# Layer 1's attention by key head, in 64 fixed steps that are filled with projections

## The chip, the core and the metric

One Trainium2 chip, one of its cores. The core has a matrix engine (TensorE, called PE here), a vector engine (DVE), a scalar engine (ACT), GpSimd (POOL) and SyncE (SP, which issues most DMAs here). The operands lie in SBUF, the results of PE in PSUM. The metric is the time of one execution on the device in microseconds (us); the kernel before takes 1667.85 us, the median of three runs (1666.11 to 1668.38).

## What is computed

A two-layer encoder over 512 tokens of width 1024. Each layer is a token mixer, a normalisation, then a mixture of 32 experts of which every token uses two. Layer 0's mixer is neighbourhood attention and is the same in both kernels. Layer 1's mixer, which the change rewrites, is grouped-query attention: 16 query heads of 64 share 4 key heads, so one key head serves four query heads.

```
def gqa_mixer(h, cos, sin, w_qkv, q_gain, k_gain, w_o):
    B, S, D = h.shape
    kvd = GQA_KV_HEADS * HEAD_DIM
    qkv = h @ w_qkv
    q = qkv[..., :D].reshape(B, S, N_HEADS, HEAD_DIM)
    k = qkv[..., D:D + kvd].reshape(B, S, GQA_KV_HEADS, HEAD_DIM)
    v = qkv[..., D + kvd:].reshape(B, S, GQA_KV_HEADS, HEAD_DIM)
    q = apply_axial_rope(rms_norm(q, q_gain), cos, sin)
    k = apply_axial_rope(rms_norm(k, k_gain), cos, sin)
    return block_gqa_attention(q, k, v) @ w_o
...
        s = jnp.einsum('bqkgd,bskd->bkgqs', qb, k).astype(jnp.float32) * scale
        p = jax.nn.softmax(s, axis=-1).astype(v.dtype)
        return jnp.einsum('bkgqs,bskd->bqkgd', p, v)
...
        x = layer_norm(DEEPNORM_ALPHA * x + (1 + g1) * y, ln_g[i, 0], ln_b[i, 0])
        h = x * (1 + sc2) + sh2
        y = hierarchical_moe(h, moe_w_group[i], moe_b_group[i], moe_w_expert[i], moe_b_expert[i],
                             moe_w_gate[i], moe_w_up[i], moe_w_down[i])
        x = layer_norm(DEEPNORM_ALPHA * x + (1 + g2) * y, ln_g[i, 1], ln_b[i, 1])
```

## The kernel before

Tokens come in four blocks `t` of 128; X[t] is a block of the residual, 128 tokens by 1024. Products that need more than one pass of the engine's precision are made of three: a weight or an activation is split into a high and a low part (`wh`/`wl`, `hTH`/`hTL`, `oH`/`oL`), the high part by a copy on ACT (L312 in `split`, L467 in `split_wo`), the low part by a subtraction on POOL or DVE (L313, L469), and PE makes high by high, high by low and low by high. Whoever splits a weight therefore gives ACT a copy and POOL a subtraction.

Layer 1 in order, with the time at which each part starts in the profile:

- From 872.9 us, `mixer1` (L718): eight steps `k` transpose a piece of the hidden state and multiply it with the first half of the key and value weights into four accumulators named `pj` (PSUM, four buffers), 12 matmuls a step; then `proj(("kv", 1))` makes the values with another 96 matmuls.
- From 906 us, four times `proj(("q1", c))`, 96 matmuls each, one for each key head `c`. `rope` (L764) takes every accumulator to SBUF on ACT and DVE, `root` (L779) makes the factor of the RMS norm on DVE and ACT, and `queries` (L808) multiplies, splits (`hf`), transposes and copies to `qS` (named w in the trace, L820). The old residual is scaled by two rows (`pg`, `pb`, broadcast by PE into PSUM) on DVE in the same stretch (L834, L835, two of them for each half of a block).
- From 981.5 us, `attention(t)` (L847) for each block `t`: 16 tiles a block, each two score matmuls (`ps`), the row maximum on DVE (`st`, L860), the exponential on ACT (`pr`, L862), four transposes on PE (`pt`) and a copy of them to SBUF (`PT`) by ACT (L869) or DVE (L867), half each. After eight tiles the probabilities multiply the values (`po`), and `scaled` (L882) divides by the sums `rz` (`rze` transposed on PE, `rzb` copied by ACT). `split_wo` (L452) is called after the first block's code, with four steps of four ACT copies and four POOL subtractions. `project(t - 1)` (L976) multiplies the block before with the output weights (`pw`, 48 matmuls), adds it to X, transposes X and makes the router's logits; `router(t - 1)` follows.
- At 1164.4 us the first expert's `gate_up` (L1375, `gu`) begins, and the mixture of experts fills the rest to 1651 us.

The order in which PE takes all this in layer 1's mixer is not written out: the list scheduler of the language interleaves the blocks by its own costs. In the mixture of experts PE's order is the program's (`manual_schedule`, L1284), SP's order is the program's everywhere. SP loads weights into slots of 1 MB (`W`, L242), a slot being free once the last reader of its weights is done.

Of the kernel before, what the change touches and what calls it, by code (L numbers as in the profile page):

```python
# [8 lines left out]
F32 = mybir.dt.float32  # L9
# [8 lines left out]
P = 128  # L18
# [16 lines left out]
NWY = (3, 1)  # L35
# [30 lines left out]
class Trunk:  # L66
# [15 lines left out]
    def plan(self):  # L82
# [50 lines left out]
        for l in range(DEPTH):  # L133
# [5 lines left out]
            for h in range(2):  # L139
                for kh in range(2):  # L140
                    add(("wo", l, h, kh), a["wo"][l, h, kh])
            for h in range(2):
                for kh in range(2):
                    add(("wl", l, h, kh), None)
# [307 lines left out]
    def split_wo(self, l, pool):  # L452
        nc = self.nc
        self.nh, self.wh = self.slots(l, pool), pool
        hk = [(h, kh) for h in range(2) for kh in range(2)]
# [262 lines left out]
    def mixer1(self, st, qS):  # L718
        nc, a, tc = self.nc, self.a, self.tc
        qv = st.enter_context(tc.tile_pool(reuse_waits="tile", name="qv1", bufs=1))  # L720
        kHL = [qv.tile([P, 4, S], F32R, name=n) for n in ("kHH", "kLL")]
        V = qv.tile([P, NT, 256], F32, name="V")
        with tc.tile_pool(reuse_waits="tile", name="m1", bufs=1) as pool, tc.tile_pool(reuse_waits="tile", name="m1p", bufs=2, space=PSUM) as pp:
            rt = pool.tile([P, 4, NT, HD], F32, name="rt")
            nc.scalar.dma_start(rt[:, 0:2], a["rope"])
            gn = pool.tile([P, 4, HD], F32, name="kk", bufs=6)
            for i in range(4):
                nc.scalar.dma_start(gn[:, i, :], bcast(a["gain"][i:i + 1], [P, HD]))
            for i in (2, 3, 0, 1):
                nc.gpsimd.tensor_tensor(rt[:, i], rt[:, i % 2], bcast(gn[:, i:i + 1, :], [P, NT, HD]), op=OP.mult)  # L730
            hH = pool.tile([P, KD, S], F32R, name="hTH")
            hL = pool.tile([P, KD, S], F32R, name="hTL")
            c1 = pool.tile([P, 2, KD], F32, name="c1")
            self.fold_cols(c1[:, 0], c1[:, 1], self.lnc[:, 0, 2], self.lnc[:, 0, 3], self.col[1][:, 0], self.col[1][:, 1])
            w = self.W(("kv", 0))
            whl = [self.split(pool, w[:, 1024 * x:1024 * x + 1024], [P, 1024], 4, (nc.vector, None)[x]) for x in range(2)]
            acc = [pp.tile([P, 4, HD], F32, name="pj", bufs=4) for t in range(NT)]
            for k in range(KD):
# [51 lines left out]
            def keys():  # L790
                r = root(ks.rearrange("p a b -> p (a b)"), 1.0, NT, "rs")
                for t in range(NT):
                    nc.vector.tensor_tensor(kk[t], kk[t], bcast(r[:, t, :, None], [P, 4, HD]), op=OP.mult)
                    kd = pool.tile([P, 2, 4, 2, HD], F32R, name="kd", bufs=1)
                    for d in range(2):
                        nc.scalar.activation(kd[:, 0, :, d, :], kk[t], AF.Copy)
# [28 lines left out]
            for c in range(4):  # L825
# [11 lines left out]
                for t, ps in proj(("q1", c)):  # L837
# [3 lines left out]
                    if t == QPOST:  # L841
                        post()
# [793 lines left out]
```

## Time and profile before

| | us |
|---|---|
| median of three runs | 1667.85 |
| the profiled execution, its own time | 1673.29 |
| its span | 1671.6 |
| PE busy in the span | 1574.7 (94%) |
| DVE busy | 700.6 (42%) |
| ACT busy | 437.6 (26%) |
| POOL busy | 162.3 (10%) |
| layer 1's mixer, first matmul to first `gu` | 872.9 to 1164.4 |

All stretches are in us from the start of the span. A busy PE is not a PE at its peak: matmuls are pipelined, and a row's duration overlaps the next row, so the price of a matmul is read from the start of one row to the start of the next. The names left and right of the arrow are tiles of the program, output first. Line numbers are those of the kernel before.

### The profile page before, as it was taken

How to read it: one execution, taken by the hardware profiler on the slowest of the kernel's cores; microseconds unless marked ns; L12 is line 12 of the kernel's file. 1: busy time of each engine (PE TensorE's matmuls, PEld its weight loads, DVE VectorE, ACT ScalarE, POOL GpSimd, SP SyncE). 2: the span in 40 equal slices, each digit the busy share in tenths (PEclk: the TensorE clock that was granted, in tenths of full speed). 3: DMA queues.
4: the chain of work that ended last, by engine and by line, in shares of the span. 5: the costliest groups of instructions: out<-in, count | busy, mean ns of one | idle time of the engine just before them, and what ended most of it. 6: DMA issues, size and time to landing. Idle time of an engine off the chain costs nothing. (4 is left out here: it accounts for less than half of the span.)

```text
span 1671.6 us, 21362 instructions
## 1 busy us (share of the span) xinstructions
PE 1574.7 (94%) x8490; PEld 906.6 (54%) x8490; DVE 700.6 (42%) x1605; ACT 437.6 (26%) x934; POOL 162.3 (10%) x99
## 2 busy tenths in 40 slices
PE   7899997989999999999979989998999999999995
PEld 4676664773544545455448866766354545545442
DVE  3434545574232322323256865666432232323235
ACT  2343335231110111111134475453011111101112
POOL 2322212010000000000014250011000000000001
PEclk9999997999999999999989989999999999999997
DMA  9587872357999999999932000035899999999981
GB/s 328 196 309 269 331 306 104 137 202 295 417 419 420 419 419 420 419 419 420 420 125 102 26 1 25 1 125 206 368 416 420 420 420 420 419 420 420 419 332 51
DMA packets 76198, 493.17 MB, mean 295 GB/s; under 512 B 9876, under 2 KB 11284, under 8 KB 18876
## 3 DMA queue, kind: packets, MB, share of 16 engines
q1 hardware_dynamic: 71916, 485.05, 71.4%
q10 hardware_dynamic: 4176, 6.69, 1.2%
q8 instruction: 69, 1.13, 0.3%
q14 instruction: 37, 0.30, 0.1%
HBM read 489.61 MB, written 2.10 MB: 294 GB/s over the span
## 5 line engine op out<-in xcount | busy, mean ns | idle before, releaser
L300 PE MATMUL gu<-w,xT 128*64 128x512 f32 x2048 | 445.0, 592 | 0.0
L300 PEld LDWEIGHTS gu<-w,xT 128*64 128x64 f32 x2048 | 146.8, 137 | 291.6 <-issue 287.0
L300 PE MATMUL pd<-w,hx 128*64 128x512 f32 x1024 | 228.0, 598 | 0.0
L1391 DVE TENSOR_TENSOR h<-h,gu 128x512 f32<-128x512 f32 x32 | 22.0, 688 | 370.4 <-PE gu L300 370.4
L300 PEld LDWEIGHTS pd<-w,hx 128*64 128x64 f32 x1024 | 70.9, 137 | 140.3 <-issue 136.7
L300 PE MATMUL gc<-OH,zH 128*128 128x256 f32 x480 | 121.5, 291 | 2.6 <-DVE OH L1276 2.6
L300 PE MATMUL gc<-OH,zL 128*128 128x256 f32 x480 | 118.6, 284 | 0.0
L300 PE MATMUL gc<-YH,OT 128*128 128x512 f32 x244 | 104.2, 427 | 1.0 <-DVE X L1358 1.0
L1358 DVE TENSOR_TENSOR X<-X,gc 128x512 f32<-128x512 f32 x128 | 87.4, 688 | 39.3 <-PE gc L300 39.3
L300 PEld LDWEIGHTS gc<-OH,zH 128*128 128x128 f32 x480 | 92.5, 193 | 14.9 <-issue 11.4
L300 PE MATMUL gc<-YL,OT 128*128 128x512 f32 x244 | 96.3, 394 | 0.0
L300 PEld LDWEIGHTS gc<-OH,zL 128*128 128x128 f32 x480 | 92.6, 193 | 0.0
L300 PE MATMUL pw<-w,oH 128*128 128x512 f32 x256 | 86.3, 408 | 0.0
L1414 ACT ACTIVATE YH<-h 128x512 fp32r<-128x512 f32 x32 | 20.2, 630 | 233.6 <-DVE h L1413 233.6
L300 PE MATMUL pj<-wh,hTH 128*128 128x256 f32 (+1 forms) x272 | 71.2, 304 | 9.1 <-ACT hTH L419 4.0
L1294 ACT ACTIVATE xT<-gc,A 128x256 f32<-128x256 f32 x60 | 33.8, 566 | 173.9 <-PE gc L300 173.9
L300 PE MATMUL pj<-wl,hTH 128*128 128x256 f32 (+1 forms) x272 | 68.0, 292 | 0.0
L300 PE MATMUL pj<-wh,hTL 128*128 128x256 f32 (+1 forms) x272 | 65.6, 293 | 0.8 <-DVE hTL L427 0.8
L300 PEld LDWEIGHTS gc<-YH,OT 128*128 128x128 f32 x244 | 45.8, 188 | 37.3 <-DVE X L1358 15.8
L1292 DVE TENSOR_SCALAR xT<-gc,A 128x256 f32<-128x256 f32 x60 | 32.5, 545 | 76.9 <-ACT xT L1294 76.5
L1390 ACT ACTIVATE h<-gu 128x512 f32<-128x512 f32 x32 | 19.1, 597 | 173.0 <-PE gu L300 173.0
L303 PE MATMUL pt<-c_ident,pr 128*128 128x128 f32 x384 | 59.5, 283 | 2.1 <-ACT pr L862 2.0
(345 smaller groups left out, 2355.9 us busy)
## 6 DMA issues: line engine op xcount, KB each, us to landing
w<-in_gu SPq DMA_DIRECT2D x256, 1024.0 KB, 14.3
w<-in_dn SPq DMA_DIRECT2D x128, 1024.0 KB, 13.5
w<-in_ada SPq DMA_DIRECT2D x40, 1024.0 KB, 7.9
wq<-in_wqk SPq DMA_DIRECT2D x16, 512.0 KB, 3.6
w<-in_wo SPq DMA_DIRECT2D x8, 1024.0 KB, 5.8
w<-in_adaq SPq DMA_DIRECT2D x6, 1024.0 KB, 12.0
bias<-in_nab ACTq DMA_DIRECT2D x24, 256.0 KB, 3.4
w<-in_wq SPq DMA_DIRECT2D x4, 1024.0 KB, 4.9
```

The lines of the kernel that those rows point to most:

```text
L300: return self.nc.tensor.matmul(out, l, r, start=start, stop=stop, **kw)
L303: self.nc.tensor.transpose(out, in_, self.ident)
L1292: nc.vector.tensor_scalar(xT[q][:, k, :], ps, s, b, op0=OP.mult, op1=OP.add)
L1294: nc.scalar.activation(xT[q][:, k, :], ps, AF.Identity, scale=s, bias=b)
L1358: nc.vector.tensor_tensor(X[t][:, c], X[t][:, c], ps, op=OP.add)
L1390: nc.scalar.activation(h, gu[0], AF.Silu)
L1391: nc.vector.tensor_tensor(h, h, gu[1], op=OP.mult)
L1414: nc.scalar.activation(YH[j][:, c], y, AF.Copy)
```

## The change

`mixer1` is written anew, and layer 1's `attention` and the old `project` are gone. The key and value weights are both split first and multiplied in one loop of eight steps with 24 matmuls each; the tables for `rope` are loaded by SP's queue in place of ACT's. Then PE's order is the program's through the whole mixer. The query projections of key heads 0 and 1 come first, with the keys and the queries of head 0 among the second. 64 steps follow, ordered by key head, block, tile (`n` = 16`c` + 4`t` + `j`). In step `n` PE makes the scores of tile `n + 2`, some fill, the transposes of tile `n`, and more fill. The fill is the query projection of head `c + 2` while `c` is 0 or 1 (8 matmuls a step) and, from step 36, the first half of the output projection (5 a step); the three first steps of every head have none. `finish` weighs the values with four tiles at a time. `pj` has two buffers instead of four.

`late()` stands at step 32, once the last query projection is done and its operands' memory is free: it splits all output weights (16 ACT copies, 16 POOL subtractions), broadcasts the row `g1` and the two rows that scale the residual, which now go to SBUF as `gb` by four ACT copies; DVE scales the residual from there (L1030, L1031 of the new file). The rest of the output projection, the four blocks' transposes and logits and the routers come after the 64 steps. Output weights are loaded in another order, three slots of 1 MB instead of one stay with the mixture of experts' `wy`, and X gets the projection's two halves in two additions.

```diff
-NWY = (3, 1)
+NWY = (3, 3)
...
+            hk = [(h, kh) for kh in range(2) for h in range(2)] if l else [(h, kh) for h in range(2) for kh in range(2)]
...
-            nc.scalar.dma_start(rt[:, 0:2], a["rope"])
...
+    def mixer1(self, st, qs, nq, pp, o, late, halves):
...
+        nc.sync.dma_start(rt[:, 0:2], a["rope"])
...
+        acc = [[pp.tile([P, 2, 256], F32, name=n, bufs=b) for _ in range(2)] for n, b in (("pj", 2), ("ps", 3))]
+        px = [self.transp(0, pp, "pt")]
+        for k in range(KD):
+            self.put_hT(k, px[k], hH, hL, c1[:, 0], c1[:, 1], pool, k % 4 == 1)
+            if k + 1 < KD:
+                px.append(self.transp(k + 1, pp, "pt"))
+            c = slice(256 * (k % 4), 256 * (k % 4) + 256)
+            for m in range(3):
+                h = hL if m == 2 else hH
...
+                        self.mm(acc[n][t // 2][:, t % 2, :], h[:, k, 128 * t:128 * t + 128], kv[n][k // 4][m == 1][:, c],
+                                k == 0 and m == 0 and t % 2 == 0, k == KD - 1 and m == 2 and t % 2 == 1)
...
+        def project(c):
+            ss[c], qq[c] = sums4(), []
+            for t in range(NT):
+                ps = pp.tile([P, 4, HD], F32, name="pj", bufs=2)
+                po = ps.rearrange("p h d -> p (h d)")
+                for k in range(KD):
+                    b = slice(256 * (k % 4), 256 * (k % 4) + 256)
+                    wh, wl = hl[c][1 + k // 4]
+                    for h, x in ((hH, wh), (hH, wl), (hL, wh)):
+                        self.mm(po, h[:, k, 128 * t:128 * t + 128], x[:, b], k == 0 and h is hH and x is wh, k == KD - 1 and h is hL)
+                        if h is hL and t == NT - 1 and k % 4 == 3:
+                            ahead(c + 1, k // 4)
+                        if k < KD - 1 or h is hH:
+                            yield
+                qq[c].append(rope(ps, t, 0, ss[c]))
+                yield
...
-                    pg = pp.tile([P, F], F32, name="pg", bufs=1)
...
-                    pb = pp.tile([P, F], F32, name="pb", bufs=1)
...
-                    nc.vector.tensor_tensor(x, x, pg, op=OP.mult)
...
-                    nc.vector.tensor_tensor(x, x, pb, op=OP.add)
...
+        def weigh(u):
+            c = u // 4
+            po[u] = pp.tile([P, 2, P], F32, name="po", bufs=1)
+            for kt in range(NT):
+                for y in range(2):
+                    self.mm(po[u][64 * y:64 * y + 64], V[:, kt, 64 * c:64 * c + 64], PT[u][:, kt, 2 * y:2 * y + 2, :],
+                            kt == 0, kt == 3)
...
+        ahead(0, 0)
+        ahead(0, 1)
+        it = project(0)
+        run(it, 96)
+        it = project(1)
+        for t in range(NT):
+            run(it, 12)
+            keys(t)
+        for t in range(NT):
+            run(it, 12)
+            queries(0, t)
+        scores(0)
+        scores(1)
+        for n in range(64):
+            c, i = n // 16, n % 16
+            if i == 0:
+                if c < 2:
+                    it = project(c + 2)
+                elif c == 2:
+                    hqs.close()
+                    late()
+                    it = halves()
+                else:
+                    self.free.append(nq)
+            if n == 24:
+                self.router_weights(1, pp)
+            k = 0 if i < 3 or n < 36 and c > 1 else 8 if c < 2 else 5
+            if n + 2 < 64:
+                scores(n + 2)
+            run(it, k - k // 2)
+            turn(n)
+            if c < 3 and 2 <= i < 6:
+                queries(c + 1, i - 2)
+                if c == 2 and i == 5:
+                    rps.close()
+            run(it, k // 2)
+            if n % 4 == 1 and n > 4:
+                finish(n // 4 - 1)
+        self.free.append(nq)
+        return it, lambda: finish(15)
...
+            def gain1():
+                lg, g1 = wk.tile([P, NT, 36], F32, name="lg"), wk.tile([P, D], F32, name="g1")
+                for h in range(2):
+                    ps = pp.tile([P, F], F32, name="pj")
+                    self.row(ps, l, 4 + h)
+                    nc.vector.tensor_scalar(g1[:, 512 * h:512 * h + 512], ps, 1.0, None, op0=OP.add)
+                return lg, g1
...
-                y = wk.tile([P, F], F32, name="y")
+                y = self.mod[0] if l else wk.tile([P, F], F32, name="y")
+                if l and kh == 0:
+                    nc.vector.tensor_tensor(x, x, gb[:, 0, c], op=OP.mult)
+                    nc.vector.tensor_tensor(x, x, gb[:, 1, c], op=OP.add)
                 nc.vector.tensor_tensor(y, pw, g1[:, c], op=OP.mult)
-                nc.vector.scalar_tensor_tensor(x, x, ALPHA, y, op0=OP.mult, op1=OP.add)
+                if l:
+                    nc.vector.tensor_tensor(x, x, y, op=OP.add)
+                else:
+                    nc.vector.scalar_tensor_tensor(x, x, ALPHA, y, op0=OP.mult, op1=OP.add)
+                yield
...
+                def late():
+                    nonlocal w, step, wk, lg, g1, gb
+                    whp = right("wh", 4)
+                    wk = right("wk", 1, rs)
+                    w, step = self.split_wo(l, whp)
+                    for _ in range(4):
+                        step()
+                    lg, g1 = gain1()
+                    gb = wk.tile([P, 2, D], F32, name="gb")
+                    for n in range(2):
+                        for h in range(2):
+                            ps = pp.tile([P, F], F32, name="pj")
+                            self.row(ps, 0, 16 + 2 * n + h)
+                            nc.scalar.activation(gb[:, n, 512 * h:512 * h + 512], ps, AF.Copy, scale=ALPHA)
+
+                def halves():
+                    for t in range(NT):
+                        for h in range(2):
+                            yield from sums(t, h, 0)
+                    for t in range(NT):
+                        for h in range(2):
+                            yield from sums(t, h, 1)
+
+                def run(n):
+                    for _ in range(n):
+                        next(it, None)
+                        made[0] += 1
+
+                w = step = wk = lg = g1 = gb = None
+                with tc.manual_schedule(engines={mybir.EngineType.PE}):
+                    it, finish = self.mixer1(st, qs, nq, pp, o, late, halves)
+                    made = [5 * 28]
+                    run(120 + 8 - made[0])
+                    hx = turnX(0)
+                    run(6)
+                    logits(0, lg[:, 0, :], hx)
+                    finish()
+                    run(144 - made[0])
+                    for t in range(1, NT):
+                        run(6)
+                        hx = turnX(t - 1) if t > 1 else None
+                        run(8)
+                        if t > 1:
+                            logits(t - 1, lg[:, t - 1, :], hx)
+                        run(4)
+                        if t != 2:
+                            self.router(t // 2, wk, pp, "pt", lg[:, t // 2, :], rt)
+                        run(6)
+                    self.router(NT - 2, wk, pp, "pt", lg[:, NT - 2, :], rt)
```

**ACT at the end of the query projections and the start of attention, before.** w is an output weight's high part where the source is w too (L467), pr an exponential, PT the copy of transposes.

```order
L467 ACTIVATE w_7923<-w_6534 128x512 x4
L467 ACTIVATE w_7932<-w_6657 128x512 x3
L862 ACTIVATE pr,rz<-ps,st 128x512 x3
L869 ACTIVATE PT<-pt 128x4x128
L467 ACTIVATE w_7932<-w_6657 128x512
L467 ACTIVATE w_7942<-w_6896 128x512
L869 ACTIVATE PT<-pt 128x4x128
L862 ACTIVATE pr,rz<-ps,st 128x512 x3
L467 ACTIVATE w_7942<-w_6896 128x512
L869 ACTIVATE PT<-pt 128x4x128
L467 ACTIVATE w_7942<-w_6896 128x512
L862 ACTIVATE pr,rz<-ps,st 128x512
```

Seven copies of weights stand ahead of the first three exponentials here, and the others come singly between exponentials and copies of transposes.

**ACT at step 32, after** (L466 is the copy that is L467 before, L864 the exponential, L874 the copy of transposes, L1112 the copy of a scaling row).

```order
L874 ACTIVATE PT<-pt 128x4x128
L466 ACTIVATE w_8146<-w_6330 128x512 x3
L466 ACTIVATE w_8155<-w_6663 128x512 x4
L466 ACTIVATE w_8165<-w_6792 128x512 x4
L466 ACTIVATE w_8175<-w_7064 128x512 x4
L1112 ACTIVATE gb<-pj 128x512 x2
L285 ACTIVATE rsr<-rst 128x16
L286 ACTIVATE rsr<-rsr 128x16
L1112 ACTIVATE gb<-pj 128x512 x2
L844 ACTIVATE hf<-kk 128x4x64 x2
L874 ACTIVATE PT<-pt 128x4x128
L864 ACTIVATE pr,rz<-ps,st 128x512
```

Before, the exponentials stand between copies of weights; now 15 copies of weights and four of `gb` stand in a row ahead of the 33rd copy of transposes and the 35th exponential (tile 34).

**DVE at step 32, after**: g is the row `g1`, X a block of the residual, kk the queries of head 3, st the row maximum of a tile.

```order
L998 TENSOR_SCALAR g_8186<-pj 128x512
L283 TENSOR_SCALAR rst<-vrs 128x16
L1030 TENSOR_TENSOR X_63<-X_63,gb 128x512 x2
L291 TENSOR_TENSOR rsu<-rsr 128x16
L1030 TENSOR_TENSOR X_64<-X_64,gb 128x512
L292 TENSOR_TENSOR rsu<-rsu,rst 128x16
L1030 TENSOR_TENSOR X_64<-X_64,gb 128x512
L293 TENSOR_SCALAR rsu<-rsu 128x16
L1030 TENSOR_TENSOR X_65<-X_65,gb 128x512
L295 TENSOR_TENSOR rsr<-rsr,rsu 128x16
L1031 TENSOR_TENSOR X_63<-X_63,gb 128x512
L842 TENSOR_TENSOR kk<-kk,rsr 128x256 x3
L862 TENSOR_REDUCE st<-ps 128x1
```

Six operations on X, which wait for `gb` from ACT, and the queries' root now stand ahead of the row maximum of tile 34; before, the same operations on X read `pg` and `pb` among the query projections.

**PE at step 32, after**: pj on c_indc are the broadcast rows, ps the scores, pt transposes, po the product with the values.

```order
L299 MATMUL ps<-kLL,w_7692 128x512
L302 MATMUL pt<-c_ident,pr 128x128 x4
L299 MATMUL pj<-mod_68,c_indc 128x512 x2
L299 MATMUL pj<-mod_67,c_indc 128x512 x4
L299 MATMUL ps<-kHH,w_7692 128x512
L299 MATMUL ps<-kLL,w_7692 128x512
L302 MATMUL pt<-c_ident,pr 128x128 x4
L299 MATMUL ps<-kHH,w_7692 128x512
L299 MATMUL ps<-kLL,w_7692 128x512
L302 MATMUL pt<-c_ident,pr 128x128 x4
L302 MATMUL pt<-c_ident,rze 128x128 x2
L299 MATMUL po<-PT,V 64x256 x8
```

The scores of tile 34 stand behind the six broadcasts that `late()` brought, of which the last two wait for a buffer that ACT's first copies of `gb` release; between here and the product `po` there is no fill.

## Rows read from the trace of the kernel before

**Rows 1.** Busy time by stretch: PE, PE's weight loads, other engines, granted clock, DMA.

```profile
core 0: us, PE busy (x) PEld busy (x) DVE busy (x) ACT busy (x) POOL busy (x), PEclk, DMA share, GB/s
872.90:878.90 6.00, 5.99 (x28) 5.99 (x29) 3.67 (x4) 4.64 (x6) 5.92 (x5) 0.50 0.06 10
878.90:906.00 27.10, 23.59 (x190) 22.33 (x190) 14.92 (x36) 13.50 (x24) 10.31 (x7) 1.00 0.33 115
906.00:968.00 62.00, 58.99 (x476) 55.39 (x474) 51.85 (x156) 27.41 (x67) 16.61 (x9) 1.00 0.10 35
968.00:981.50 13.50, 10.97 (x52) 9.10 (x51) 5.87 (x24) 6.04 (x17) 0.71 (x1) 0.62 0.01 2
981.50:1122.20 140.70, 138.51 (x714) 88.18 (x712) 88.46 (x199) 84.54 (x207) 28.39 (x23) 1.00 0.07 27
1122.20:1164.40 42.20, 34.87 (x205) 29.52 (x204) 29.28 (x90) 14.31 (x30) 11.24 (x5) 0.96 0.64 260
1140.40:1151.40 11.00, 9.85 (x48) 8.13 (x48) 6.08 (x18) 1.74 (x5) 0.00 (x0) 0.84 0.98 403
1300.00:1600.00 300.00, 300.00 (x1544) 147.29 (x1543) 88.71 (x169) 41.39 (x81) 0.00 (x0) 1.00 1.01 419
```

**Rows 2.** Waits of SP's queue, whole span: us in total, times, longest.

```profile
SPq L272 <- PE pd L300: 385.4, 61, 16.4
```

**Rows 3.** Timeline of PE (start, us, group): prices of one matmul from start to start.

```profile
894.25 0.28 PE L300 MATMUL pj<-wl,hTH 128*128 128x256 f32 x1
894.36 0.28 PE L300 MATMUL pj<-wh,hTL 128*128 128x256 f32 x1
...
985.23 0.60 PE L303 MATMUL pt<-c_ident,pr 128*128 128x128 f32 x4
985.59 0.47 PE L300 MATMUL ps<-kLL,w 128*128 128x512 f32 x1
985.90 0.40 PE L300 MATMUL ps<-kHH,w 128*128 128x512 f32 x1
...
995.26 3.65 PE L300 MATMUL po<-PT,V 128*64 128x512 f32 x14
998.84 0.33 PE L303 MATMUL pt<-c_ident,rze 128*128 128x128 f32 x1
```

**Rows 4.** Groups by line, 960 to 1130: busy, mean ns of one, idle before.

```profile
L862 ACT ACTIVATE pr<-ps,st 128x512 f32<-128x512 f32 x64 | 43.7, 689 | 10.4 <-DVE st L860 9.3 <-ACT pr L862 0.7 <-PE pt L303 0.2
L860 DVE TENSOR_REDUCE st<-ps 128x1 f32<-128x512 f32 x64 | 42.4, 683 | 8.6 <-PE ps L300 8.3
L469 POOL TENSOR_TENSOR w<-w,w 128x512 fp32r<-128x512 f32 x16 | 20.1, 1286 | 38.0 <-issue 37.7
L869 ACT ACTIVATE PT<-pt 128x512 f32<-128x512 f32 x32 | 19.1, 598 | 16.7 <-PE pt L303 16.2
```

**Rows 5.** Timeline of ACT: the weight copies ahead of the first exponential.

```profile
980.04 3.74 ACT L467 ACTIVATE w<-w 128x512 fp32r<-128x512 f32 x7
```

**Rows 6.** Timeline of POOL, one weight subtraction among the key projections.

```profile
893.89 2.40 POOL L313 TENSOR_TENSOR wl<-w,wh 128x1024 fp32r<-128x1024 f32 x1 [5.24 <-ACT wh L312]
```

**Rows 7.** Timeline of DVE in `rope` and `root` of the keys.

```profile
894.46 2.12 DVE L789 TENSOR_TENSOR kk<-t,t 128x256 f32<-128x256 f32 x1
896.50 0.41 DVE L770 TENSOR_TENSOR t<-pj,rt 128x256 f32<-128x256 f32 x1
...
897.55 0.41 DVE L789 TENSOR_TENSOR kk<-t,t 128x256 f32<-128x256 f32 x1
897.89 0.41 DVE L770 TENSOR_TENSOR t<-pj,rt 128x256 f32<-128x256 f32 x1
...
900.45 0.17 DVE L284 TENSOR_SCALAR rst<-vrs 128x16 f32<-128x16 f32 x1
...
901.99 1.09 DVE L793 TENSOR_TENSOR kk<-kk,rsr 128x256 f32<-128x256 f32 x3
```

**Rows 8.** Timeline of PE behind a router's wait, in the tail.

```profile
1140.48 0.18 PE L300 MATMUL pt<-Mb,trib 128*128 128x32 bf16 x1 [2.35 <-DVE Mb L1126]
```

More of the change, by code (lines that the diff above doesn't have):

```diff
@@ new lines, in mixer1 @@
+        rps, hqs = ExitStack(), ExitStack()
+        pool, hq = rps.enter_context(left("rp1")), hqs.enter_context(left("hq1"))
+        rt = pool.tile([P, 4, NT, HD], F32, name="rt")
+        nc.sync.dma_start(rt[:, 0:2], a["rope"])
+        gn = pool.tile([P, 4, HD], F32, name="kk", bufs=8)
+        for i in range(4):
+            nc.sync.dma_start(gn[:, i, :], bcast(a["gain"][i:i + 1], [P, HD]))
+        hH = hq.tile([P, KD, S], F32R, name="hTH")
+        hL = hq.tile([P, KD, S], F32R, name="hTL")
@@ new lines, in root, with sums4 @@
+        def root(ss, extra, n, tag):
+            v = pool.tile([P, n * 4], F32, name="v" + tag, bufs=2)
+            nc.vector.tensor_scalar(v, ss, 1.0 / HD, None, op0=OP.mult)
+            return self.rstd(pool, v, n * 4, RMS_EPS, extra, tag).rearrange("p (a b) -> p a b", a=n)
+        def sums4():
+            return pool.tile([P, NT, 4], F32, name="ss", bufs=3)
+        ks = sums4()
+        kk = [rope(acc[0][t // 2][:, t % 2, :].rearrange("p (h d) -> p h d", h=4), t, 1, ks) for t in range(NT)]
@@ new lines, in close, with rest @@
+        def close(u):
+            z = rz[u]
+            nc.vector.reciprocal(z, z)
+            e = at.tile([P, 2, 2, 64], F32, name="rze", bufs=1)
+            nc.vector.tensor_copy(e, bcast(z.rearrange("p (y x) -> p x y", y=2)[:, :, :, None], [P, 2, 2, 64]))
+            pt = pp.tile([P, 2, P], F32, name="pt")
+            for x in range(2):
+                self.tr(pt[:, x, :], e[:, x].rearrange("p a b -> p (a b)"))
+            r = at.tile([P, 2, P], F32, name="rzb", bufs=1)
+            nc.scalar.activation(r, pt, AF.Copy)
+            def rest():
+                nc.vector.tensor_tensor(r, po[u], r, op=OP.mult)
+                oH, oL = o[u // 4, u % 4] = [oq.tile([P, 2, P], F32R, name=n, bufs=10) for n in ("oH", "oL")]
+                nc.scalar.activation(oH, r, AF.Copy)
+                nc.gpsimd.tensor_tensor(oL, r, oH.bitcast(F32), op=OP.subtract)
+            return rest
@@ new lines, in finish, with run @@
+        def finish(u):
+            rest = close(u)
+            weigh(u)
+            rest()
+        def run(it, n):
+            for _ in range(n):
[22 more added lines that the diff above has]
+                    it = halves()
+                else:
+                    self.free.append(nq)
[13 more added lines that the diff above has]
+                finish(n // 4 - 1)
```

350 lines of the change are left out of this document (124 added, 226 removed).

## The prediction

> **What bounds the kernel now.** I read the stretches first. From the first `gu` on PE is the bound: in 300 us of the experts it is busy for 300.00 us at full clock [rows 1]. The DMA engines are as full there (1.01), so the next view was SP's queue: on the down projections alone it waits 385.4 us for PE to free a slot [rows 2]. Loads follow PE and not the reverse, and the first experts' slots come free when the attention ends, in both kernels. So what layer 1's mixer, 872.9 to 1164.4, gains or loses arrives at the end whole. Nothing behind 1164.4 changes in work.
>
> Inside the mixer PE is also the bound nearly everywhere. Idle or slowed time is what a new order could save, and the stretches tell how much there is: 3.5 us in the key and value projections (27.10 less 23.59), 3.0 in the query projections (62.00 less 58.99), and a slow place of 13.5 us, 968 to 981.5, in which PE did 10.97 us of work at a granted clock of 0.62; that is 6.8 us of work at full clock, so 6.7 are lost there. Attention has only 2.2 us of idle (140.70 less 138.51), the tail 7.3 (42.20 less 34.87) [rows 1]. In all some 23 us, of which no order gets all.
>
> **What the change keeps.** The passes of PE are the same: 384 query matmuls and 192 for keys and values at 0.11 to 0.12 us, 64 tiles of two scores (0.31 for the first; some 0.25 for the second, as the records of `po`, of as many columns) and four transposes (0.36), 128 `po` instructions of 256 columns for 64 of 512 (two records each in the trace; 14 records take 3.58 us), as many output matmuls [rows 3]. What is moved is work at the same price in another place, and I price only waits and clock. The three extra `wy` slots and the other order of output weights change loads in a stretch where DMA has a share of 0.07 [rows 1]; zero, covered by the attention itself; if that cover were gone the output weights would arrive late for step 32, which the rows give no sign of.
>
> **Keys and values in one loop: -4 us.** The start keeps 6.00 us at half clock (0.50), which does 3.0 us of work [rows 1]. The loop's work is 192 matmuls at 0.1175, 22.6, and eight groups of transposes at 0.36, 2.9: 25.5 in all [rows 3]. So it takes 6.0 + 22.5, with 0.6 for stalls 29.1, where the two stretches took 33.1. Bounds: 0 if ACT's and DVE's splits of the hidden state pace it as before, -4.6 without stalls. The tables' loads leave ACT's queue for SP's; SP waits there for PE anyway.
>
> **Query projections 0 and 1, keys, queries 0: -4 us.** Before, 3.0 idle and 6.7 lost to the low clock, 9.7 in all. After, the first query projection needs one of now two `pj` buffers, which the key accumulators hold until `rope` has taken two blocks: two at 1.39 us (896.50 to 897.89), with the square and the sum of the first ahead of them, some 3.9 us of wait [rows 7]. A split weight of head 1 comes late from POOL by about 2 us (one subtraction is 2.40 us [rows 6]), and 0.7 for the next buffer: 6.6, an estimate. That leaves 3 to be gained, or more if the keys' transposes take less than now; I take -4, between 0 and -7.
>
> **The 64 steps without step 32: +6 us.** A tile on ACT is an exponential of 0.69 with its read of the sum and, for three tiles of four, a copy of 0.60 [rows 4], about 1.4 in a chain. On PE a tile is 0.56 for scores, 0.36 for transposes and, by the records of `po`, about 0.5 for its share of that and 0.1 for `rze`; with 8 query matmuls (0.94) that is some 2.4 us, with 5 output matmuls (1.25) some 2.7: PE is the longer one, and ACT and DVE are hidden. Not hidden is the start: the first maximum, exponential, transposes and copy in a row are 0.68 + 0.69 + 0.36 + 0.60 = 2.3 [rows 3, 4], and the root for head 1's queries, asked for at step 2, is a chain of 1.5 us to its end and 1 more to the products (900.45 to 903) [rows 7], behind the squares of a projection that has just ended: some 4. Two us more at the change of head and at the router's weights make 8.5, where attention now idles 2.2. Bounds +2 to +10.
>
> **The tail: +3 us.** All four blocks' transposes and logits and three routers now lie behind the steps, with 67 output matmuls among them; before, two of the routers lay inside attention. One wait for a router was 2.35 us [rows 8], and the 11 us behind it ran at a clock of 0.84 [rows 1]. One more of these, partly covered: +3, from 0 to +6.
>
> **Step 32: +20 us, and this decides.** Call T0 the end of the transposes of tile 31. ACT then has 15 weight copies in a row before anything of the attention; seven took 3.74 us [rows 5], so 15 take 8.0. Behind them stand the four copies to `gb`, the root's two steps and two `hf`, about 3 us. Only then come the copy of tile 32's transposes and the exponential of tile 34. On DVE the maximum of tile 34 stands behind six operations on X that wait for `gb`, at about 0.6 each, the root, and three `kk`. On PE the broadcasts hold the scores of tile 34 until ACT has copied the first of `gb`. So PE has its broadcasts, two scores and two groups of transposes, about 4.7 us, and then nothing: there is no fill until step 36. With every engine at its own pace tile 34's exponential is done at about T0 + 14.6, and PE loses some 10 us. Before, the same 16 copies cost little because nine of them lay between exponentials, as the order of ACT above shows, and the first seven were part of the slow place.
>
> POOL makes it worse. It has 16 subtractions of 1.286 us in a row from T0 [rows 4], so about eight are left when `gb` is there. Where such a subtraction ran beside a DVE operation that reads two SBUF tiles, DVE waited for its end: `kk` took 2.12 us beside POOL's 2.40, from 894.46 to 896.58, and 0.41 three us later without it; POOL's one ended at 896.29 [rows 6, 7]. The nine operations ahead of tile 34's maximum (six on X, three `kk`; a factor that is spread over columns is an SBUF tile too) are of this kind. Each then waits for one subtraction until POOL is through: eight times 1.27 is 10 us more. Before, X was scaled by rows in PSUM, and during its 16 subtractions DVE read PSUM. The sum is 10 without this effect, 20 with it; I take 20, since the row is of the same pair of operations, and keep 8 to 27.
>
> The Trainium skill, "SBUF — State Buffer", section "Who interferes with whom", says that DVE and GpSimd share one pair of SBUF ports as an exclusive lock, that a DVE instruction with two SBUF inputs contends with a GpSimd instruction that reads SBUF, and that issue order decides who blocks. By that rule each of the nine would wait, as in my sum; the row of 2.12 us agrees, and without the rule the step would cost 10.
>
> **Clock: +1.5 us.** Behind an idle of 2.35 us the tail's clock was 0.84 over 11 us, a loss of 1.8 [rows 1, 8]. The gap here is longer. I take 1.5, from 0 to 4.
>
> **Sum.** -4 - 4 + 6 + 3 + 20 + 1.5 = +22.5. The profiled execution took 1673.3, so its like would take 1695.8; the median of the runs is 5.4 lower, 1667.85, and gives 1690.4.
>
> **Rivals.**
> - The flood without the lock: step 32 costs 10, the sum is +12.5 and the time about 1680. For it: POOL may be through sooner, if its first subtractions run before T0. Against it: 16 at 1.286 are 20.6 us and cannot end before the operations on X are due.
> - Faster: the waits at step 32 stay under 8 us since output weights and rows are handled while the last query projection still fills PE, and the two places before the steps give what their idle time holds. Then -4.6 - 7 + 2 + 0 for the parts and about 1 for the rest: -8.6, so about 1659. It decides whether ACT's 15 copies start by step 29, 8 us earlier. Against it: the order of ACT puts one copy ahead of the exponential of tile 33 and 15 behind tile 31's transposes.
> - No change: step 32 costs what the parts ahead of it gain, about 1668. It needs the 8 to 10 us of copies to lie half beside other work and no lock.
> - Worse: POOL also delays `oL`, whose buffer `rzb` the next `finish` needs, or the two `pj` buffers starve the fill; +35, about 1703.
>
> **How the numbers follow.** Forecast 0.52, flood without lock 0.20, faster 0.12, no change 0.08, worse 0.08. The forecast's own range is 1683 to 1698. The range of 8 in 10 takes the second case in and reaches to 1668 below and 1701 above; it leaves out the faster case, half of no change and most of worse. About 0.2%, or 3.3 us, is what a measurement of this kernel can tell from no change: faster 0.12, same 0.08, slower 0.80.
>
> **What would show it.** The key and value loop ends about 902 and the first scores start about 938 to 942, both earlier than now. At step 32 a gap of PE of 10 us or more, ended by ACT, with 15 weight copies ahead of the copies to `gb`; the operations on X far above 0.6 us while POOL subtracts, and about 0.6 if the rival is right. `gu` starts at 1187, and from there the traces agree with a shift. I am wrong if PE has no gap of over 5 us in the steps, or if the first `gu` is moved and the end is not.

## The result, and the profile after

The changed kernel takes 1694.75 us, the median of four runs (1693.38 to 1696.37), beside 1667.19 for the kernel before, the median of four as well: a ratio of 1.0166, 95% interval 1.0148 to 1.0183, or 27.6 us more. The forecast was 1690.4.

The profiled execution of after has a span of 1691.6 us, only 20.0 more than that of before. The two differ by 5.8 us already when layer 1 begins (PE's last matmul of layer 0 starts at 861.22 before and at 855.41 after), and that part of the program is the same in both. It is a draw of the executions: the kernel before with an edit in layer 1 alone, measured below, starts PE's first transposes of layer 1 at 860.02, where the kernel before itself starts them at 867.85. All that follows is therefore measured inside the mixer, from PE's first transposes of layer 1 to the first `gu`: 296.5 us before (867.85 to 1164.38), 322.4 after (862.03 to 1184.44), 25.9 more. Behind the first `gu` both have 507.2 us left to the end of the span, so the shift is passed on whole.

Busy time by stretch of the changed kernel; the columns are those of [rows 1].

```profile
866.70:894.50 27.80, 27.80 (x216) 27.62 (x216) 15.23 (x15) 8.07 (x12) 10.63 (x7) 0.90 0.21 77
894.50:932.20 37.70, 30.56 (x242) 29.88 (x241) 29.09 (x87) 17.42 (x42) 10.97 (x8) 0.95 0.16 57
932.20:1024.60 92.40, 83.29 (x580) 69.79 (x579) 55.30 (x135) 55.08 (x137) 13.67 (x11) 0.91 0.04 12
1024.60:1057.10 32.50, 17.73 (x67) 9.27 (x66) 25.19 (x38) 18.44 (x42) 23.69 (x17) 0.79 0.00 1
1057.10:1134.00 76.90, 76.06 (x470) 58.29 (x468) 49.16 (x101) 41.33 (x101) 5.12 (x7) 1.00 0.04 15
1134.00:1184.40 50.40, 37.87 (x219) 33.16 (x215) 40.28 (x147) 17.89 (x44) 10.54 (x5) 0.83 0.66 271
1300.00:1600.00 300.00, 300.00 (x1544) 145.32 (x1542) 88.27 (x173) 41.40 (x81) 0.00 (x0) 1.00 1.01 419
```

These are the key and value loop, the query projections up to the first scores, steps 0 to 31, step 32 up to the first output matmul, the filled steps, the tail, and the experts as in [rows 1]. PE is full in the loop, in the filled steps and in the experts. It is not in the fourth stretch: 17.73 of 32.50 us, at a clock of 0.79.

The timeline of PE shows the gaps (start, duration, group, idle before and its releaser):

```profile
898.00 0.36 PE L299 MATMUL pj<-wh,hTH 128*128 128x256 f32 x1 [3.48 <-DVE t L776]
913.43 0.39 PE L299 MATMUL pj<-wl,hTH 128*128 128x256 f32 x1 [2.04 <-POOL wl L312]
943.14 1.09 PE L302 MATMUL pt<-c_ident,hf 128*128 128x128 f32 x4 [4.10 <-DVE hf L845]
1034.85 3.78 PE L299 MATMUL pj<-mod,c_indc 128*128 128x512 f32 x4 [5.55 <-ACT gb L1112]
1048.92 0.69 PE L302 MATMUL pt<-c_ident,rze 128*128 128x128 f32 x2 [8.09 <-ACT PT L874]
1161.15 0.18 PE L299 MATMUL pt<-Mb,trib 128*128 128x32 bf16 x1 [5.40 <-DVE Mb L1214]
```

Six gaps make 28.7 of the mixer's idle time. The two of step 32 are 13.6. Here are ACT, DVE and POOL in the same place, each from its own timeline:

```profile
1026.40 7.91 ACT L466 ACTIVATE w<-w 128x512 fp32r<-128x512 f32 x15
1034.20 1.08 ACT L1112 ACTIVATE gb<-pj 128x512 f32<-128x512 f32 x2
1048.29 0.58 ACT L874 ACTIVATE PT<-pt 128x512 f32<-128x512 f32 x1
...
1034.83 3.27 DVE L1030 TENSOR_TENSOR X<-X,gb 128x512 f32<-128x512 f32 x2 [6.39 <-ACT gb L1112]
1038.02 1.24 DVE L291 TENSOR_TENSOR rsu<-rsr 128x16 f32<-128x16 f32 x1
1039.18 0.68 DVE L1030 TENSOR_TENSOR X<-X,gb 128x512 f32<-128x512 f32 x1
1039.79 1.24 DVE L292 TENSOR_TENSOR rsu<-rsu,rst 128x16 f32<-128x16 f32 x1
...
1045.05 4.29 DVE L842 TENSOR_TENSOR kk<-kk,rsr 128x256 f32<-128x256 f32 x3
1049.26 0.68 DVE L862 TENSOR_REDUCE st<-ps 128x1 f32<-128x512 f32 x1
...
1027.13 21.92 POOL L468 TENSOR_TENSOR w<-w,w 128x512 fp32r<-128x512 f32 x15 [0.35 <-ACT w L466]
1039.19 1.80 POOL L468 TENSOR_TENSOR w<-w,w 128x512 fp32r<-128x512 f32 x1
```

(The last row is one of the 15 above it.) The 15 copies took 7.91 us and end the first gap through `gb`. DVE then needs from 1034.83 to 1049.26, 14.4 us, for what stands ahead of the maximum of tile 34, until POOL's 15 subtractions end at 1049.05. Three `kk` take 4.29 us, where three of them took 1.09 before [rows 7], and an operation on 16 columns takes 1.24 us instead of 0.17. Of the 13 operations ahead of that maximum nine are slow in this way: the first two on X, four of the root and the three `kk`. The other four on X take 0.68 us each, beside 0.69 in the run without subtractions below. POOL pays too: 1.46 us a subtraction on average where it was 1.286 [rows 4], and 1.80 where an operation on X went ahead of it.

Splitting the mixer by what PE does gives the account below. It is worked out from the busy time of 1-us pieces: idle is length less busy, clock loss is busy time times one less the granted clock, the rest is PE's time at full clock.

| | before | after | difference |
|---|---|---|---|
| first transposes to first `gu` | 296.5 | 322.4 | +25.9 |
| PE idle | 21.7 | 47.1 | +25.4 |
| lost to the low clock | 10.1 | 21.7 | +11.6 |
| rest | 264.7 | 253.6 | -11.1 |

So PE's own time falls by 11 us, and idle time and a low clock add 37. Where the 11 us come from can be read from the starts of PE's rows, idle time left out and at the granted clock: the products with the values (`po`) take 36.7 us before, in 128 records of 512 columns, and 30.0 after, in 256 of 256; the 128 score matmuls take 37.5 and 32.9.

### The profile page after: what moved, and what is told of

Read it like the earlier page. It is cut to its first block, busy times and chain, and to the rows that moved or that the text cites. A ratio compares the mean times of both kernels' runs of the same rounds, so it can differ in the third digit from the quotient of the medians.

```text
span 1691.6 us, 21659 instructions
## 1 busy us (share of the span) xinstructions
PE 1572.1 (93%) x8618; PEld 923.7 (55%) x8618; DVE 718.3 (42%) x1616; ACT 447.8 (26%) x959; POOL 165.7 (10%) x107
## 3 DMA queue, kind: packets, MB, share of 16 engines
q8 instruction: 70, 1.15, 0.3%
## 5 line engine op out<-in xcount | busy, mean ns | idle before, releaser
L299 PE MATMUL pj<-w,oH 128*128 128x512 f32 x256 | 87.2, 409 | 0.7 <-DVE g L998 0.7
L299 PE MATMUL pj<-wh,hTH 128*128 128x256 f32 (+1 forms) x240 | 63.4, 312 | 9.4 <-DVE t L776 3.5
L1478 ACT ACTIVATE h<-gu 128x512 f32<-128x512 f32 x32 | 19.1, 597 | 173.0 <-PE gu L299 173.0
L299 PE MATMUL pj<-wl,hTH 128*128 128x256 f32 (+1 forms) x240 | 60.5, 301 | 2.0 <-POOL wl L312 2.0
L862 DVE TENSOR_REDUCE st<-ps 128x1 f32<-128x512 f32 x64 | 44.0, 689 | 38.5 <-PE ps L299 37.9
```

The lines of the kernel that those rows point to most:

```text
L299: return self.nc.tensor.matmul(out, l, r, start=start, stop=stop, **kw)
L862: nc.vector.tensor_reduce(s[:, 0:1], ps, axis=AX.X, op=OP.max, negate=True)
L1478: nc.scalar.activation(h, gu[0], AF.Silu)
```

## Experiments

Each is an edit of the changed kernel unless it says otherwise. "Mixer" is the stretch of 296.5 and 322.4 us above, taken from one profile each. The kernel before and its edit below, which agree in time, differ by 2 us in it (296.5 and 294.5) with the same idle time, so 2 us of mixer show nothing by themselves.

**POOL's subtractions left out.** This is the direct test of the blocking.

```diff
-                eng = nc.gpsimd if l or k % 2 else nc.vector
-                eng.tensor_tensor(wL[z][:, c], x[:, c], wH[z][:, c].bitcast(F32), op=OP.subtract)
+                eng = nc.gpsimd if k % 2 else nc.vector
+                if not l:
+                    eng.tensor_tensor(wL[z][:, c], x[:, c], wH[z][:, c].bitcast(F32), op=OP.subtract)
+            if l:
+                nc.gpsimd.memset(wL[z].bitcast(F32), 0.0)
```

> The changed kernel, but POOL fills the low parts of layer 1's output weights with zeros in four instructions instead of 16 subtractions (the low parts are left out of the result); ACT's copies and DVE's operations stay as they are. Theory: nothing blocks DVE, its operations on X take about 0.65 us each and the chain to the maximum of tile 34 shortens from 14 to some 5 us: about 1685, 1683 to 1688; the gap that ACT's copies make, about 5.5 us, stays. Rival (no blocking, the operations are slow or ACT is the cause): 1694, no change.

Measured: 1682.7 us, ratio 1.0098 (1.0081 to 1.0115); mixer 311.5, 10.9 less. From the timelines of PE and DVE:

```profile
1035.24 3.78 PE L299 MATMUL pj<-mod,c_indc 128*128 128x512 f32 x4 [5.55 <-ACT gb L1115]
...
1035.22 1.29 DVE L1033 TENSOR_TENSOR X<-X,gb 128x512 f32<-128x512 f32 x2 [6.62 <-ACT gb L1115]
1039.17 1.09 DVE L845 TENSOR_TENSOR kk<-kk,rsr 128x256 f32<-128x256 f32 x3
1040.18 0.68 DVE L865 TENSOR_REDUCE st<-ps 128x1 f32<-128x512 f32 x1
```

The gap that ACT ends is the same 5.55 us. DVE's chain falls from 14.4 to 5.0 us (1035.22 to 1040.18), two operations on X from 3.27 to 1.29, and the gap of 8.09 is gone. The blocking is shown, at 11 us of mixer, 8.4 of them idle time of PE; the gap that the copies on ACT make stays.

**The same in the kernel before**, where DVE reads PSUM during these subtractions.

```diff
-                eng.tensor_tensor(wL[z][:, c], x[:, c], wH[z][:, c].bitcast(F32), op=OP.subtract)
+                if not l:
+                    eng.tensor_tensor(wL[z][:, c], x[:, c], wH[z][:, c].bitcast(F32), op=OP.subtract)
+            if l:
+                nc.gpsimd.memset(wL[z].bitcast(F32), 0.0)
```

> The kernel before, with POOL's 16 subtractions of the output weights replaced by four fills with zeros (the low parts are left out of the result). Theory: DVE reads PSUM in that stretch and is not blocked, so 1667, within 2 us. Rival (POOL's subtractions cost time wherever they are): 1657 to 1662.

Measured: 1669.3 us, ratio 1.0000 (0.9986 to 1.0014). The same subtractions cost the kernel before nothing, though they stand in a row there too:

```profile
980.79 20.29 POOL L469 TENSOR_TENSOR w<-w,w 128x512 fp32r<-128x512 f32 x16 [37.75 <-issue]
```

Beside them DVE makes row maxima from PSUM at 0.68 us each, which is also their mean over the whole attention [rows 4]. The price lies in what DVE does beside the subtractions.

**Output weights split in three places.**

```diff
+            if n in (40, 48):
+                more()
...
-                    for _ in range(4):
+                    for _ in range(2):
```

> The changed kernel, but only the two output weights of the first half are split at step 32; the other two are split at steps 40 and 48. Theory (ACT's 15 copies in a row and POOL's 16 subtractions in a row, which block DVE's two-input operations, make the loss of about 20 us at step 32): ACT reaches the copies of gb some 4 us earlier, and POOL has about 4 instead of 8 subtractions left when DVE scales X, so 5 us more: about 1685 us, 1682 to 1689. Rival (the copies alone, no blocking): about 1690, and DVE's operations on X take 0.6 us in both kernels.

Measured: 1692.34 us, ratio 1.0159 (1.0142 to 1.0176); mixer 317.5, 4.9 less. A gain is not shown: the interval overlaps that of the changed kernel, and PE's idle time in the mixer is 46.8 us where it was 47.1, so the 4.9 are clock, in one profile. The first gap falls from 5.55 to 1.43, but DVE is still blocked, and the wait only moves to the queries:

```profile
1029.72 1.98 PE L299 MATMUL pj<-mod,c_indc 128*128 128x512 f32 x4 [1.43 <-ACT gb L1114]
1049.95 1.12 PE L302 MATMUL pt<-c_ident,hf 128*128 128x128 f32 x4 [12.00 <-DVE hf L845]
...
1029.70 4.10 DVE L1032 TENSOR_TENSOR X<-X,gb 128x512 f32<-128x512 f32 x3 [2.24 <-ACT gb L1114]
1042.39 4.23 DVE L842 TENSOR_TENSOR kk<-kk,rsr 128x256 f32<-128x256 f32 x4
...
1026.14 19.34 POOL L468 TENSOR_TENSOR w<-w,w 128x512 fp32r<-128x512 f32 x13 [0.35 <-ACT w L466]
```

I had expected POOL to have half as many subtractions left. It did not: the scheduler took the later splits forward among the exponentials of the tiles just behind step 32 (ACT's last weight copy ends at 1045.84), and POOL went on subtracting beside DVE.

**The residual scaled from PSUM, before step 32.**

```diff
+            if n in (17, 22, 25, 28):
+                scale((17, 22, 25, 28).index(n))
...
-                            nc.scalar.activation(gb[:, n, 512 * h:512 * h + 512], ps, AF.Copy, scale=ALPHA)
+                def scale(m):
+                    ps = pp.tile([P, F], F32, name="pj")
+                    self.row(ps, 0, 16 + 2 * (m % 2) + m // 2)
+                    for t in range(NT):
+                        x = X[t][:, 512 * (m // 2):512 * (m // 2) + 512]
+                        nc.vector.tensor_tensor(x, x, ps, op=(OP.mult, OP.add)[m % 2])
```

> The changed kernel, but the residual is scaled from rows in PSUM, as in the kernel before, at steps 17, 22, 25 and 28; the copies to gb and the six operations on X are gone from step 32, the 16 weight copies and subtractions stay there. Theory: the first gap of PE, which the copies of gb end, shrinks only by the two copies, but six of the nine blocked operations are gone, some 8 us: about 1686, 1683 to 1690. Rival (the copies alone): 2 to 3 us less than the changed kernel, about 1692. A second rival, that DVE is then too full in steps 17 to 31: about 1695.

Measured: 1696.12 us, ratio 1.0175 (1.0158 to 1.0192); mixer 323.5. A miss: no gain. The operations on X are gone from step 32, but the wait of 11.50 us at the queries has two causes. ACT's two steps of the root stand behind the 15 copies and come at 1048.37; from there POOL blocks the root's products and the `kk` until its 15 subtractions end at 1056.63. The queries of head 2 wait 4.3 us behind a DVE that scales X.

```profile
991.00 1.11 PE L302 MATMUL pt<-c_ident,hf 128*128 128x128 f32 x4 [4.32 <-DVE hf L845]
1057.92 1.09 PE L302 MATMUL pt<-c_ident,hf 128*128 128x128 f32 x4 [11.50 <-DVE hf L845]
...
1050.09 1.19 DVE L292 TENSOR_TENSOR rsu<-rsu,rst 128x16 f32<-128x16 f32 x1
1052.67 4.24 DVE L842 TENSOR_TENSOR kk<-kk,rsr 128x256 f32<-128x256 f32 x3
...
1037.38 19.25 POOL L468 TENSOR_TENSOR w<-w,w 128x512 fp32r<-128x512 f32 x15 [0.35 <-ACT w L466]
```

Taking some of the victims away while the subtractions stay lets the next ones be caught.

**Both edits.**

> Both edits, weights split at steps 32, 40 and 48 and the residual scaled from PSUM. Theory: most of the 20 us of step 32 is gone, about 1678, 1675 to 1682, still 10 us above the kernel before, since the start of the steps and the tail stay. Rival (copies alone): about 1688.

Measured: 1690.13 us, ratio 1.0136 (1.0119 to 1.0153); mixer 316.7. The wait at the queries is 5.42 us, that of head 2 is still 4.32. Less than expected, in part by the cause of the two runs above: the root's first two products take 1.15 and 1.19 us beside the subtractions, while four `kk` behind them take 1.43 in all and are not blocked.

**The queries four steps later.**

```diff
-            if c < 3 and 2 <= i < 6:
-                queries(c + 1, i - 2)
-                if c == 2 and i == 5:
+            if c < 3 and 6 <= i < 10:
+                queries(c + 1, i - 6)
+                if c == 2 and i == 9:
```

> The changed kernel, but the queries of heads 1, 2 and 3 are normalised, split and transposed four steps later (steps 6 to 9 of a head instead of 2 to 5). Theory: the gap of 4.1 us at the start of the steps and the half clock behind it go, 6 to 9 us; and of the operations that POOL blocks at step 32 the root and the three kk leave, 3 to 5 us: about 1683, 1679 to 1688. Rival (the chain of the root waits for DVE and POOL wherever it stands): 1692 to 1695, with the gap at another step.

Measured: 1690.56 us, ratio 1.0131 (1.0110 to 1.0153); mixer 313.6, 8.8 less. The first scores to the end of tile 31's transposes take 86.0 us instead of 92.5; the gap of 4.10 is gone, and the clock losses of that stretch fall from 6.4 to 3.4. At step 32 little is gained (gaps of 5.56 and 7.57), since the scheduler left the root and one of the three `kk` ahead of the maximum on DVE and put a seventh operation on X there.

**Four edits together**: both above, the queries later, one split at step 32, the others at 35, 43 and 50, and an even fill.

```diff
-            k = 0 if i < 3 or n < 36 and c > 1 else 8 if c < 2 else 5
+            k = 6 if c < 2 else 0 if n < 36 or i < 3 else 5
```

> Four edits together: output weights split at steps 32, 35, 43 and 50, the residual scaled from PSUM, the queries four steps later, and six query matmuls in every step of heads 0 and 1 instead of eight in thirteen of sixteen. Theory: step 32 costs at most 4 us and the start of the steps 2, so about 1674, 1669 to 1679, still above the kernel before by the tail. Rival (losses move to another step, as the edit of the residual did): 1682 to 1688.

Measured: 1677.74 us, ratio 1.0052 (1.0032 to 1.0072); mixer 302.5, 19.9 less than the changed kernel and 6 more than before. No gap of step 32 is over 1.5 us. What is left lies in the tail (a gap of 5.40), in steps 16 to 31 (four of 1.1 to 1.9) and, as in the changed kernel, ahead of and in the first query projections (3.48 and 2.04).

**Later matmuls between the routers.**

```diff
-                        run(8)
+                        run(4)
...
-                        run(4)
...
-                        run(6)
+                        run(14)
```

> The same four edits, and in the last blocks the logits and the routers stand four and eight matmuls earlier, so that 14 instead of 6 lie between router 1 and router 2. Theory: the gap of 5.4 us ahead of router 2's first matmul shrinks by 2 us: 1.5 to 2.5 us below the kernel with four edits. Rival: the routers' chains on DVE are what is late, and the gap moves to router 1: no change.

Measured: ratio 1.0050 (1.0034 to 1.0065); mixer 303.9. No gain, as the rival said, though the gap did not move to router 1: the waits join into one of 9.81 us for DVE.

**Shorter subtractions in the tail**, on top of the four edits.

```diff
-                    nc.gpsimd.tensor_tensor(zL[t], X[t], zH[t].bitcast(F32), op=OP.subtract)
+                    for q in range(4 if l else 1):
+                        b = slice(256 * q, 256 * q + 256) if l else slice(0, D)
+                        nc.gpsimd.tensor_tensor(zL[t][:, b], X[t][:, b], zH[t][:, b].bitcast(F32), op=OP.subtract)
```

> The kernel with four edits (weights spread, residual scaled from PSUM, queries later, even fill), and POOL's subtractions that make the low part of X for the experts are cut into four pieces of 256 columns. Theory (the wait of 5.4 us ahead of router 2 is the same blocking: two DVE operations of that chain take 2.46 and 2.33 us beside a subtraction of 2.5): the gap falls to 2 or 3 us and the stretch of half clock behind it shortens, 3 to 6 us less in the mixer, about 1673. Rival (the router's own chain of small operations is late): the gap stays at 5.4, no change.

Measured: 1674.2 us, ratio 1.0034 (1.0020 to 1.0048); mixer 300.2, 2.2 less than with four edits. The intervals of the two overlap, so a gain in time is not shown; what is shown is local. In the changed kernel the chain of router 2 met two subtractions of 1024 columns (timelines of DVE and POOL; with four edits the two rows of DVE, 2.46 and 2.33, and the gap of 5.40 are the same):

```profile
1155.94 2.46 DVE L1034 TENSOR_TENSOR X<-X,mod 128x512 f32<-128x512 f32 x1
1158.32 2.33 DVE L1058 SCALAR_TENSOR_TENSOR lg<-lg,lnr,rbs 128x36 f32<-128x36 f32 x1
...
1155.51 5.09 POOL L1158 TENSOR_TENSOR zL<-X,zH 128x1024 fp32r<-128x1024 f32 x2 [19.36 <-DVE mod L1032]
```

With pieces of 256 columns these two rows and the gap are

```profile
1138.58 0.83 DVE L1035 TENSOR_TENSOR X<-X,mod 128x512 f32<-128x512 f32 x1
1139.34 0.71 DVE L1059 SCALAR_TENSOR_TENSOR lg<-lg,lnr,rbs 128x36 f32<-128x36 f32 x1
...
1141.51 0.18 PE L299 MATMUL pt<-Mb,trib 128*128 128x32 bf16 x1 [3.12 <-DVE Mb L1218]
```

so 2.3 of the 5.4 us were the same blocking; other operations of the chain now wait 0.4 to 0.5 us each. The pieces have a price: POOL takes 5.99 us for eight of them where two whole subtractions took 5.09.

**Other buffers for the first query accumulators**, and one low part of the weights made by DVE.

```diff
-                hl[c].append(self.split(hq, hl[c][0][:, 1024 * x:1024 * x + 1024], [P, 1024], 2))
+                hl[c].append(self.split(hq, hl[c][0][:, 1024 * x:1024 * x + 1024], [P, 1024], 2, nc.vector if (c, x) == (1, 0) else None))
...
-                ps = pp.tile([P, 4, HD], F32, name="pj", bufs=2)
+                name, bufs = (("po", 1), ("ps", 3), ("pj", 2))[2 if c else min(t, 2)]
+                ps = pp.tile([P, 4, HD], F32, name=name, bufs=bufs)
```

> The same with the pieces, and two edits at the start: the first two accumulators of query projection 0 lie in the buffers of po and ps, which are free then, and the low part of the first half of head 1's query weights is made by DVE. Theory: the gap of 3.5 us behind the key and value loop goes and the one of 2.0 halves: 4 us less than the kernel with the pieces, about 1669, equal to the kernel before within its noise. Rival: the rotation on DVE is what is late, and the gaps only move to the next buffer: no change.

Measured: ratio 1.0028 (1.0016 to 1.0039); mixer 301.9. No gain: the gap of 3.48 goes and that for head 1's `wl` falls from 2.04 to 0.88, but waits for POOL's `wl` of head 0 (2.04) and for `hf` (1.76) come.

**The residual scaled earlier**, at steps 5, 9, 13 and 17 instead of 17 to 28, on top of the pieces.

```diff
-            if n in (17, 22, 25, 28):
+            if n in (5, 9, 13, 17):
```

> The kernel with four edits and the pieces, but the residual is scaled at steps 5, 9, 13 and 17, each one step behind the start of an accumulator, in place of 17, 22, 25 and 28, where the router's weights lie too. Theory (the gaps of 1.9, 1.8 and 1.5 us in steps 17 to 30 come from DVE, which holds a pj buffer for the four operations on X): two of the three go, 3 to 5 us less, about 1670, equal to the kernel before. Rival (these gaps come from the router's weights and the rotation alone): no change, 1674.

Measured: ratio 1.0035 (1.0023 to 1.0047); mixer 302.4. No gain: three gaps of 0.9 to 1.9 us move to the new steps, and the 1.8 us at the router's weights stay.

No version beat the kernel before; the best come to within 0.3%.

## Why the prediction was right, point by point

- **The bound.** Right: 300.00 us of PE in 300 and a shift passed on whole. Among the loads, too, SP still waits for PE.
- **Keys and values: -4.** The loop takes 27.8 us instead of 33.1, -5.3, and starts 0.4 earlier; a little better than the bound of -4.6, since PE's own work is 25.1 where 25.5 was counted, and the half clock cost 2.7 instead of 3.
- **Query projections: -4.** The loop's end to the first scores is 37.7 us, 41.9 before by the same subtraction of moved work: -4.2. The waits were priced one by one as 3.9, 2 and 0.7, and are 3.48, 2.04 and 0.70 to 0.91.
- **Steps 0 to 31: +6.** The step that failed in size. Idle time there is 9.1 us, and 0.8 in the filled steps, near the 8.5 of the sum, but the clock takes 6.4 more, for which the sum had nothing in these steps. The gap of 4.10 us, which I had foreseen, lies in a stretch at a clock of 0.50 that began 2 us ahead of it.
- **Step 32: +20, and +1.5 for the clock.** Right in mechanism, and near in size: 14.8 us idle and 4.3 of clock, 19.1 beside 21.5. Without the subtractions the same stretch has 6.7 and 2.1, so the two parts, 10 for the copies and 10 for the blocking, are 8.7 and 10.4 with their clock. The exponential of tile 34 was done 26.0 us after T0 (1024.64 to 1050.66), where the estimate was 14.6 and 10 more for the blocking. The sign that was named did not come as named: not one gap of 10 us but two, of 5.55 and 8.09, both ended by ACT, and of the six operations on X only two were far above 0.6. That the blocking still came to 10 was luck in part. Nine operations were counted and nine waited, but four of them are the root's small ones, 1.24 us each, which were not on the list, in place of four on X. In the run with the residual scaled from PSUM this error decided, together with ACT's copies.
- **Tail: +3.** Too small: idle and clock are 18.1 us where they were 9.0, so +9. The wait for router 2 is 5.40 instead of 2.35 [rows 8], of which 2.3 are again POOL against DVE, and the clock is 0.50 behind it. It is one more long wait, as forecast, but longer than the one that it was priced by.
- **Work the same on both sides.** Wrong: PE's own time falls by 11 us, of which 6.7 in attention and tail are not in the sum. It hides in the rows as busy time: the prices of the products with the values (14 records in 3.58 us [rows 3], 256 ns a record of 512 columns) and of the scores were taken as the same in both kernels, and these two fell, as the starts of PE's rows show. No run tells why they are cheaper in the new order. This error and those of the clock and the tail are of opposite sign, so that a sum of 22.5 met 25.9 is luck in part.
- **The end.** `gu` starts at 1184.4; with the 5.8 us by which this execution was ahead that is 1190.2, where 1187 was named, and from there the traces agree with a shift.
- **The rivals.** The flood without the lock would have been 1680; leaving the subtractions out gives 1682.7, which is that case. The faster case needed ACT's 15 copies by step 29; they started at 1026.40, behind tile 31. The four edits did by hand what it needs, and even then the tail and the steps keep the kernel behind.

The Trainium skill, "SBUF — State Buffer", section "Who interferes with whom", says that a DVE instruction with two SBUF inputs contends with a GpSimd instruction that reads SBUF. That agrees with the run without subtractions (14.4 against 5.0 us) and with the kernel before, which reads PSUM and loses nothing.

## What to carry to other kernels

When work is gathered at one step, read each engine's static order there for what stands ahead of the instruction that the bound engine needs next; where the fill has run out, a row of copies shows as a gap (7.91 us of copies, a gap of 5.55). If GpSimd subtracts from SBUF for 20 us, most of what DVE reads from two SBUF tiles in that time waits for a subtraction (eight of twelve such operations at step 32), down to operations on a few columns: put those on PSUM, keep them away, or cut the subtraction short. And price a gap of TensorE with the clock around it.

## What the runs showed of the hardware

A gap can cost more than its length. In steps 0 to 31 and behind step 32 the granted clock of the changed kernel fell to the lower of its two levels, 1.2 GHz (stretches of the same view as above):

```profile
932.20:937.00 4.80, 3.16 (x19) 2.12 (x17) 4.10 (x9) 3.63 (x9) 3.81 (x2) 1.00 0.00 0
937.00:939.00 2.00, 2.00 (x8) 1.29 (x6) 1.87 (x5) 1.38 (x4) 0.00 (x0) 0.50 0.93 287
940.00:944.00 4.00, 0.86 (x5) 0.89 (x5) 2.80 (x10) 1.41 (x6) 0.00 (x0) 0.50 0.03 12
944.00:950.00 6.00, 6.00 (x38) 5.73 (x37) 2.05 (x4) 3.81 (x9) 0.00 (x0) 0.73 0.00 0
...
1035.00:1040.00 5.00, 5.00 (x11) 2.59 (x12) 5.00 (x5) 1.80 (x5) 4.92 (x4) 0.56 0.00 0
1049.00:1053.20 4.20, 4.20 (x19) 2.02 (x19) 3.80 (x9) 1.72 (x5) 0.06 (x1) 0.52 0.01 4
```

Behind the two gaps of step 32 PE worked at 0.56 and 0.52, each time for some 4 us. The second of these stretches goes with its gap: without POOL's subtractions the gap of 8.09 is not there, and the clock is 1.00 from 1040.8 to 1053. At the start of the steps the clock fell before the long gap, when PE had been busy for 3.16 of 4.80 us, and with the queries four steps later, which takes that gap away, it stays at 1.00 there. From the same view, first without the subtractions, then with the later queries:

```profile
1040.80:1053.00 12.20, 11.04 (x74) 7.97 (x72) 11.95 (x25) 9.02 (x24) 1.45 (x1) 1.00 0.00 1
...
934.20:950.00 15.80, 14.07 (x100) 11.27 (x98) 13.99 (x38) 11.81 (x31) 4.39 (x3) 1.00 0.19 66
```

A gap of one length does not have one price: with the weights split in three places the same gap of 4.10 us stands in a stretch (939 to 943) at 0.91. In the whole mixer the low clock cost 21.7 us, almost half of what idleness cost.

The blocking caught an operation with a single SBUF input too: `rsu` by a constant (L293), 0.17 us in the run without subtractions, takes 1.23 beside them. Not every time: with the residual scaled from PSUM it took 0.17 beside them.

```profile
1041.55 1.23 DVE L293 TENSOR_SCALAR rsu<-rsu 128x16 f32<-128x16 f32 x1
...
1051.31 0.17 DVE L293 TENSOR_SCALAR rsu<-rsu 128x16 f32<-128x16 f32 x1
```
